# Per-token factors of an attention output: from widened transposes on TensorE to rows that go through DRAM

## The chip, the cores and the metric

The kernel runs on one core of a Trainium2 chip. The metric is the device time of one execution, in microseconds (us); the kernel before takes 1531.06 us in the median of three runs (1530.86 to 1531.6). TensorE is called PE here, VectorE DVE, ScalarE ACT, GpSimd POOL and SyncE SP, as in the profile. SP, ACT and POOL also issue DMAs, each in the order of its own queue.

## What is computed

Two layers of an encoder over 512 tokens with 1024 channels, in float32. Cut to what the change touches:

```python
proj = einsum('bsd,de->bse', x, w_in)                 # q, k, v of both mixers and two gates
oa, _ = banded_attention(qa, ka, va, 128, a_sink)     # mixer A: 8 heads, o / denom per token and head
ya = einsum('bse,ed->bsd', oa, w_branch_a)
for g, (window, dil) in enumerate(B_GROUPS):          # mixer B: 3 groups of 4 heads
    o, lse = dilated_attention(qb[g], kb[g], vb[g], window, dil)
wts = softmax(stack(lses), axis=0)                    # one factor per token, head and group
ob = einsum('gbsh,gbshd->bshd', wts, stack(outs))
yb = einsum('bse,ed->bsd', ob, w_branch_b)
h = einsum('bsd,de->bse', ga * ya + gb * yb, w_out)
x = layer_norm(alpha * x + h)
mlp = square(relu(x @ w_up)) @ w_down
x = layer_norm(alpha * x + mlp + sigmoid(x @ w_ple_gate + b) * (p[i] @ w_ple))
```

The change concerns the division by `denom` and the weights `wts`: a head's output `o` is kept with its 64 channels on the partitions and the 512 tokens along the row, so a factor per token has to be multiplied along the row, the same in 64 partitions.

## The kernel before

Weights come as 512 KB tiles `wst` through the SP queue into three buffers (L252), and are split into a high and a low part (`whi`, `wlo`; L236, or L240 with a POOL DMA that adds into `wlo`). Three matmuls per weight block (`mm3`, L287) make a float32 product out of the parts.

In `attention_block` (L358) PE's order is written by a planner: the loop at L854 runs small generators, each of which yields a condition on a forecast time `fc.t` and then emits the next step of a unit. Units of mixer A (`unit_a`, four per layer, two heads each) and of mixer B (`unit_b`, two spans `sp` times three groups `g`) emit scores (`sa`, `sb`), transposed probabilities (`pta`, `ptb`), and weighted values (`oa`, `ob`). Between them `filler` emits the projections (`ps_('qb', …)` and the like) and, at the end of the block, `ya`. `LEAVE` (L42) is a table by unit and step: a step listed there is put off by so many forecast microseconds after it could run. Only PE's order is fixed so; the other engines are put in order by the scheduler of the framework, which places each instruction where its own reckoning has the operands ready. Every engine and every queue then runs its list in order: what stands behind a waiting instruction waits too.

The scores of a step lie in two banks of tag `s`; DVE adds the mask into `pa` and takes the maximum (L466), which frees the bank; ACT takes the exponential (L462). Transposed probabilities go through two banks of tag `pt`, and are split by ACT and DVE. `o` is one bank, freed by `join` (L485: an ACT copy and a DVE addition).

The factors: `widened` (L493) copies a 128x8 tile of factors (tokens on the partitions) to 128x512 on ACT, 64 times each; `token_scaled` (L498) transposes its four 128x128 blocks into a `pt` bank (`rs`, L501) and DVE multiplies `f` by it (L502). A unit of mixer A does this once at its end, and `mix_b` (L704), once per span, three times, after the transposes `ex` and `ey` that bring the maxima and sums of the dilated groups into the order of the tokens. Then ACT and DVE split the result into `oah`/`oal` or `obh`/`obl`, which `ya` and `yb` read.

The embedding half `embedding(l, 0)` (L1096) for the second layer is made at the end of the first (L1358 to L1363) and kept in SBUF in the pool `p1` through the second layer's attention, until `embed` reads it. `kept` are DRAM tiles where the residual `y` waits meanwhile.

## Time and profile before

| | |
|---|---|
| profiled execution | 1530.95 us, of it 1529.2 us from the first to the last instruction |
| TensorE clock granted | 0.996 of full speed in the mean |
| attention of the first layer | about 38 to 305 us, of the second about 800 to 1068 us |
| end of the first layer, start of the second | about 750 to 790 us |
| DMA | 190.52 MB in the span, mean 125 GB/s |

Times inside the execution are microseconds from the first instruction. A matmul's duration reaches past the start of the next one, since matmuls are pipelined; what it costs PE is read from one start to the next.

### The profile page before, as it was taken

To read this page: it belongs to the slowest core of one execution; us is meant where nothing else is said; L and a number is where in the kernel's file an instruction comes from. 1 tells how busy PE (TensorE), PEld (TensorE's weight loads), DVE (VectorE), ACT (ScalarE), POOL (GpSimd) and SP (SyncE) were. 2 spreads that over 40 slices of the span, in tenths; PEclk is the share of its full clock that TensorE was granted. 3 is DMA by queue.
4 is the path that set the end of the run, shared out by engine and by line. 5 is a ranking of instruction groups with operands and counts; after the bars stand their busy time and mean duration, and the time that the engine had idled before them with its cause. 6 is when DMAs were issued, how large, how long until landed. Compare 5 with 4: busy or idle time off the path is not lost.

```text
span 1529.2 us, 19607 instructions
## 1 busy us (share of the span) xinstructions
PE 1506.9 (99%) x7374; PEld 1249.8 (82%) x7374; DVE 1030.7 (67%) x1761; ACT 768.2 (50%) x1254; POOL 250.9 (16%) x221
## 2 busy tenths in 40 slices
PE   9999999999999999999999999999999999999996
PEld 7888888888888888888888888888888888888885
DVE  5865564458568777686868655544585876767868
ACT  5887674344344443444558776643442444444342
POOL 1221220110011120202022112211100201111022
PEclk9999999999999999999999999999999999999998
DMA  7644655345612414151455456565455233231403
GB/s 243 144 109 117 147 138 191 99 138 152 206 56 86 135 53 155 42 159 62 105 169 138 113 123 150 126 188 156 150 151 181 69 110 111 85 123 56 150 0 97
DMA packets 54592, 190.52 MB, mean 125 GB/s; under 512 B 6625, under 2 KB 7009, under 8 KB 54497
## 3 DMA queue, kind: packets, MB, share of 16 engines
q1 hardware_dynamic: 43200, 151.74, 29.8%
q0 software_dynamic: 10576, 37.23, 13.0%
q8 instruction: 58, 0.95, 0.2%
q10 hardware_dynamic: 720, 0.30, 0.1%
q14 instruction: 38, 0.30, 0.1%
HBM read 155.16 MB, written 4.19 MB: 104 GB/s over the span
## 4 chain that ended last, share of the span: by engine, by line
PE 87%; DVE 6%; ACT 2%; DMA 2%; issue 2%; POOL 0%; SPq 0%; POOLq 0%; ACTq 0%; DVEq 0%
PE dn L1065 17%; PE ps_up L291 8%; PE ps_up L289 8%; PE ps_up L290 8%; PE wo L297 2%; PE pg L297 2%; PE pg L295 2%; PE pg L296 2%; PE wo L296 2%; PE wo L295 2%; PE pta L451 1%; PE sb L473 1%; PE sa L478 1%; PE ya L289 1%; PE ya L291 1%
## 5 line engine op out<-in xcount | busy, mean ns | idle before, releaser
L237 ACT CAST whi<-wst 128x1024 fp32r<-128x1024 f32 (+2 forms) x120 | 121.1, 1010 | 261.6 <-PE ps_up L290 115.4
L238 DVE TENSOR_TENSOR wlo<-wst,whi 128x1024 fp32r<-128x1024 f32 (+2 forms) x120 | 146.1, 1222 | 142.3 <-ACT whi L237 131.9
L289 PE MATMUL ps_up<-xhi,whi 128*128 128x512 f32 x512 | 199.2, 389 | 0.0
L290 PE MATMUL ps_up<-xlo,whi 128*128 128x512 f32 x512 | 199.2, 389 | 0.0
L291 PE MATMUL ps_up<-xhi,wlo 128*128 128x512 f32 x512 | 199.2, 389 | 0.0
L1038 POOL TENSOR_TENSOR hr<-r 128x512 f32<-128x512 f32 x64 | 102.2, 1597 | 550.2 <-ACT r L1030 529.7
L290 PEld LDWEIGHTS ps_up<-xlo,whi 128*128 128x128 f32 x512 | 96.1, 188 | 20.0
L291 PEld LDWEIGHTS ps_up<-xhi,wlo 128*128 128x128 f32 x512 | 96.1, 188 | 19.9
L289 PEld LDWEIGHTS ps_up<-xhi,whi 128*128 128x128 f32 x512 | 96.1, 188 | 19.9
L237 ACT CAST whi<-raw 128x1024 fp32r<-128x1024 f32 x56 | 58.0, 1052 | 97.0 <-PE ps_up L290 64.1
L237 ACT CAST dhi<-raw 128x1024 fp32r<-128x1024 f32 x56 | 58.7, 1052 | 82.2 <-PE dn L1065 59.5
L1084 DVE TENSOR_TENSOR y<-y,dn 128x512 f32<-128x512 f32 x96 | 65.2, 682 | 38.5 <-PE dn L1065 38.5
L244 POOL DMA_DIRECT2D wlo<-wst x54 | 47.8, 885 | 253.6 <-ACT wlo L243 150.9
L1018 DVE TENSOR_TENSOR raw<-raw,raw 128x1024 f32<-128x1024 f32 x64 | 86.4, 1350 | 0.2
L238 DVE TENSOR_TENSOR wlo<-raw,whi 128x1024 fp32r<-128x1024 f32 x56 | 68.2, 1220 | 14.1 <-ACT whi L237 14.1
L238 DVE TENSOR_TENSOR dlo<-raw,dhi 128x1024 fp32r<-128x1024 f32 x56 | 69.2, 1239 | 5.4 <-ACT dhi L237 5.4
L242 ACT CAST whi<-wst 128x1024 fp32r<-128x1024 f32 x54 | 56.5, 1046 | 30.3 <-PE ps_start L290 6.9
L243 ACT ACTIVATE wlo<-whi 128x1024 fp32r<-128x1024 f32 x54 | 57.3, 1061 | 0.8
L1065 PE MATMUL dn<-whi,smh 128*128 128x512 f32 x128 | 50.2, 394 | 0.7 <-DVE y L1084 0.7
L1065 PE MATMUL dn<-wlo,smh 128*128 128x512 f32 x128 | 50.5, 395 | 0.1
L1065 PE MATMUL dn<-whi,sml 128*128 128x512 f32 x128 | 49.9, 390 | 0.0
L1065 PE MATMUL dn<-dhi,smh 128*128 128x512 f32 x128 | 49.9, 390 | 0.0
(860 smaller groups left out, 4049.2 us busy)
## 6 DMA issues: line engine op xcount, KB each, us to landing
wst<-wst SPq DMA_DIRECT2D x187, 512.0 KB, 3.5
raw<-wst SPq DMA_DIRECT2D x64, 512.0 KB, 4.3
wlo<-wst POOLq DMA_DIRECT2D x54, 512.0 KB, 4.6
y<-rows POOLq DMA_DIRECT2D x14, 512.0 KB, 7.7
row<-rows SPq DMA_DIRECT2D x7, 512.0 KB, 8.4
wst<-wst SPq DMA_DIRECT2D x9, 256.0 KB, 2.7
xs<-xT SPq DMA_DIRECT2D x8, 256.0 KB, 6.2
y<-xN SPq DMA_DIRECT2D x4, 512.0 KB, 6.6
```

Source lines behind the costliest of these rows:

```text
L237: nc.scalar.copy(hi, src)
L238: nc.vector.tensor_tensor(lo, src, hi.bitcast(F32), ALU.subtract)
L289: nc.tensor.matmul(ps, w[0][:, s], x[0], start=start, stop=False, skip_group_check=part)
L290: nc.tensor.matmul(ps, w[0][:, s], x[1], start=False, stop=False, skip_group_check=part)
L291: nc.tensor.matmul(ps, w[1][:, s], x[0], start=False, stop=stop, skip_group_check=part)
L295: nc.tensor.matmul(ps, x[0], w[0][:, c], start=start, stop=False)
L296: nc.tensor.matmul(ps, x[0], w[1][:, c], start=False, stop=False)
L297: nc.tensor.matmul(ps, x[1], w[0][:, c], start=False, stop=stop)
L1018: nc.vector.tensor_tensor(to, to, other, ALU.add)
L1038: nc.gpsimd.tensor_tensor(h.rearrange("p s t -> p (s t)"), r, r, ALU.mult)
L1065: nc.tensor.matmul(ps[s], a[:, k, tok], w[b][:, cols], start=first and not (k or m), stop=k == 3 and m == 2, skip_group_check=True)
L1084: return nc.vector.tensor_tensor(to, to, ps, ALU.subtract if n in (2, 4, 5) else ALU.add)
```

## The change

For each unit of mixer A, and for each span of mixer B, one transpose turns the factors themselves (128x8, or 128x24 for three groups) into rows (`in_rows`). ACT copies the rows to SBUF and issues a DMA that writes them to a DRAM tile `line`. SP then reads a row of `line` back into 64 partitions, twice for a tile `R` of 128x512 (`in_columns`). The multiplication is taken out of the unit and put into a generator of its own on the list `side`, which waits until the forecast has passed `LATENCY` = 7 (`scaled_a`, `mixed_b`). `f` gets two buffers and `R` three; `ya` waits until all four `oa` are scaled. `LEAVE` has other entries.

The embedding half for the second layer is written to DRAM after it is made, and read back in `np1` in the second layer; no pool holds it through the attention.

```diff
+LATENCY = 7
 LEAVE = {
-    ("a", 0, 1): 0.6, ("a", 0, 14): 0.6, ("a", 1, 4): 0.3, ("a", 1, 16): 4.5, ("a", 2, 18): 1.0,
...
+    ("a", 0, 1): 2.2, ("a", 0, 11): 2.2, ("a", 0, 14): 1.5, ("a", 0, 16): 1.5, ("a", 1, 4): 1.0,
...
-            def widened(c, name, after):
-                wide = av.tile([P, 4, 2, 64], F32, tag="wide", name="wide" + name, bufs=1)
-                nc.scalar.copy(wide, c.rearrange("p r (j u) -> p j r u", u=1).to_broadcast([P, 4, 2, 64]))
-                return wide, fc.on("act", 0.52, after) + HOP
-
-            def token_scaled(f, wide, name, after):
-                R = bank("pt", "rs" + name)
-                for j in range(4):
-                    nc.tensor.transpose(R[:, j * P:(j + 1) * P], wide[:, j].rearrange("p r d -> p (r d)"), ident)
+            def in_rows(c, n, name, after):
+
+                tp = bank("pt", "rt" + name)
+                nc.tensor.transpose(tp[:n, :P], c, ident)
+                r = av.tile([24, P], F32, tag="rt", name="rt" + name, bufs=1)
+                nc.scalar.copy(r[:n], tp[:n, :P])
+                t = fc.on("act", 0.3, fc.pe(0.11) + HOP) + HOP
+                fc.take("pt", t)
+                line = dp.tile([24, P], F32, tag="line", name="line" + name, bufs=2)
+                nc.scalar.dma_start(line[:n], r[:n])
+                return line, max(t, after) + LATENCY
+
+            def in_columns(line, name):
+                R = av.tile([P, S], F32, tag="wide", name="R" + name, bufs=3)
+                for r in range(2):
+                    nc.sync.dma_start(R[r * 64:r * 64 + 64, :],
+                                      line[r * 4:r * 4 + 4].rearrange("j p -> (j p)").partition_broadcast(64))
+                return R
+
+            def scaled_a(i, f, R, t):
+                yield lambda: fc.t >= t
                 nc.vector.tensor_tensor(f, f, R, ALU.mult)
-                t = fc.on("dve", 0.6, max(fc.pe(0.43) + HOP, after)) + HOP
-                fc.take("pt", t)
-                return t
+                split(OA[i][0], OA[i][1], f)
+                forecast_split(S, fc.on("dve", 0.7, fc.t))
+                del held["oa", i]
+
+            def mixed_b(sp, fs, Rs, t):
+                yield lambda: fc.t >= t
+                for (f, _, _), R in zip(fs, Rs):
+                    nc.vector.tensor_tensor(f, f, R, ALU.mult)
+                f = fs[0][0]
+                nc.gpsimd.tensor_tensor(f, f, fs[1][0], ALU.add)
+                nc.vector.tensor_tensor(f, f, fs[2][0], ALU.add)
+                split(OB[sp][0], OB[sp][1], f)
...
-                yield lambda: fc.open("pt") and fc.t >= t_wide
-                t_f = token_scaled(f, wide, nm_, t_f)
-                split(OA[i][0], OA[i][1], f)
-                forecast_split(S, t_f)
+                yield lambda: fc.open("pt") and fc.t >= t_den
+                line, t = in_rows(den.rearrange("p r j -> p (r j)"), 8, nm_, t_f)
+                side.append([scaled_a(i, f, in_columns(line, nm_), t), None, ("oa", i), 0])
...
+                yield lambda: fc.t >= t and fc.open("pt")
+                line, t = in_rows(e.rearrange("p g b -> p (g b)"), 24, nm_, t)
+                Rs = [in_columns(line[8 * g:8 * g + 8], f"{nm_}_{g}") for g in range(3)]
+                side.append([mixed_b(sp, fs, Rs, t), None, ("ob", sp), 0])
...
-                        yield lambda: not any(k[0] == "a" for k in (*waiting, *live))
+                        yield lambda: not any(k[0] in ("a", "oa") for k in (*waiting, *live, *held))
...
+        kept_ple = [dp.tile([P, S], F32, tag=f"keptple{a}", name=f"keptple{a}", bufs=1) for a in range(4)]
...
+            for a in range(4 if l else 0):
+                ple[0, a] = np1.tile([P, S], F32, tag="ple0", name=f"ple{l}_0_{a}", bufs=4)
+                nc.sync.dma_start(ple[0, a], kept_ple[a])
...
+                    for a in range(4):
+                        nc.sync.dma_start(kept_ple[a], ple[0, a])
```

What this makes of the engines' lists is shown at three places, first before, then after the change.

The first place is PE's list where the first span's weights of mixer B are turned (first layer, second span under way). `rs_0_0` are the widened transposes, `rt_0` is the one transpose of the changed kernel; `ps_('vb', 1, 1)` and `ps_('qb', 1, 2)` are projections of the filler. Before:

```order
L483 MATMUL ob_1_0_0_2137<-ptlb_1_0_1_2068,vvvb_1_0_1927 64x2x128
L501 MATMUL rs_0_0_2166<-ident,wide_0_0_2102 128x128 x4
L289 MATMUL ps_('vb', 1, 1)_2124<-xhi,whi_1896 128x512
L290 MATMUL ps_('vb', 1, 1)_2124<-xlo,whi_1896 128x512
L291 MATMUL ps_('vb', 1, 1)_2124<-xhi,wlo_1897 128x512
L451 MATMUL ptb_1_0_3_2177<-ident,pb_1_0_1_1954 128x128 x4
```

After:

```order
L293 MATMUL ps_('vb', 1, 1)_2113<-xhi,wlo_1906 128x512
L498 MATMUL rt_0_2156<-ident,e_0_2045 24x128
L291 MATMUL ps_('qb', 1, 2)_2180<-xhi,whi_1997 128x512
L292 MATMUL ps_('qb', 1, 2)_2180<-xlo,whi_1997 128x512
L293 MATMUL ps_('qb', 1, 2)_2180<-xhi,wlo_1998 128x512
```

Before, three groups of four transposes stand within 23 rows of the list, the first of them shown; now one row stands there, between products of the filler.

The second place is DVE's list around the multiplication of mixer A's unit 1 (first layer). `pa_3_…<-sa_3_…` are the masks of unit 3's scores, `ptla_2_…` the low halves of unit 2's probabilities. Before:

```order
L466 ISA pa_3_1_994,mxa_3_995<-sa_3_0_1_1000,ct_157 128x256
L466 ISA mxa_3_995 128x1
L502 TENSOR_TENSOR fa_1_716<-fa_1_716,rsa_1_985 128x512
L532 SCALAR_TENSOR_TENSOR nma_3_996<-mxa_3_995,nsk_160 128x2
L238 TENSOR_TENSOR ptla_2_0_1019<-pta_2_0_1013,ptha_2_0_1018 128x512
L466 ISA pa_3_0_993,mxa_3_995<-sa_3_1_0_1049,ct_157 128x384
```

After:

```order
L240 TENSOR_TENSOR ptla_2_1_1043<-pta_2_1_1038,ptha_2_1_1042 128x384
L468 ISA pa_3_0_996,mxa_3_998<-sa_3_1_0_1052,ct_158 128x384
L468 ISA mxa_3_998 128x1
L516 TENSOR_TENSOR fa_1_713<-fa_1_713,Ra_1_993 128x512
L468 ISA pa_3_1_997,mxa_3_998<-sa_3_1_1_1053,ct_158 128x384
L468 ISA mxa_3_998 128x1
L555 SCALAR_TENSOR_TENSOR nma_3_999<-mxa_3_998,nsk_161 128x2
L240 TENSOR_TENSOR oal_152<-fa_1_713,oah_151 128x512
L240 TENSOR_TENSOR ptla_2_2_1079<-pta_2_2_1074,ptha_2_2_1078 128x384
```

The multiplication now reads `Ra_1`, which two DMAs bring, and stands between the masks of the two banks of `sa_3_1`; before, it read the bank that PE had just written.

The third place is SP's queue between the layers, with the writes of `y` and of the embedding half and the load of the constants `ct` for the second layer's attention. Before:

```order
L1355 DMA kept_136<-y_0_2869 128x1024
L366 DMA ct_6775<-cst 128x1920
L1355 DMA kept_137<-y_1_2870 128x1024
L258 DMA wst_6704<-wst 128x1024
L258 DMA wst_6839<-wst 128x1024
```

After:

```order
L1374 DMA kept_136<-y_0_2866 128x1024
L1374 DMA kept_137<-y_1_2867 128x1024
L1384 DMA keptple_140<-ple_0_0_6468 128x512
L260 DMA wst_6704<-wst 128x1024
L1384 DMA keptple_141<-ple_0_1_6477 128x512
L260 DMA wst_6840<-wst 128x1024
L1384 DMA keptple_142<-ple_0_2_6518 128x512
L1384 DMA keptple_143<-ple_0_3_6527 128x512
L368 DMA ct_6776<-cst 128x1920
```

`ct` has moved behind the four writes of the embedding half and two loads of weights.

## The prediction

> **What bounds the kernel now.** The page's busy times come first.

> ```profile
> PE 1506.9 (99%) x7374; PEld 1249.8 (82%) x7374; DVE 1030.7 (67%) x1761; ACT 768.2 (50%) x1254; POOL 250.9 (16%) x221
> ```

> Then the shares of the chain that ended last, by engine:

> ```profile
> PE 87%; DVE 6%; ACT 2%; DMA 2%; issue 2%; POOL 0%; SPq 0%; POOLq 0%; ACTq 0%; DVEq 0%
> ```

> PE is busy for 1506.9 of 1529.2 us, so the time falls only by work taken off PE or by its waits. The view of who waited for whom, for PE alone, gives the waits:

> ```profile
> PE ps_start L291 <- DMA wlo<-wst: 1.5, 1, 1.5
> ...
> PE sa L478 <- DVE mxa L466: 0.9, 2, 0.5
> ...
> PE rs L501 <- ACT wide L495: 0.8, 2, 0.4
> PE ptb L451 <- ACT pb L462: 0.4, 2, 0.2
> ```

> None is above 1.5 us. A late result costs more than the idle time shown, since the pipeline runs dry too; so I read costs from one start to the next, in PE's timeline; first around the first group of widened transposes:

> ```profile
> 71.94 0.34 PE L483 MATMUL oa<-ptla,vvva 128*64 128x384 f32 x1
> 72.12 0.60 PE L501 MATMUL rsa<-ident,widea 128*128 128x128 f32 x4
> 72.47 0.36 PE L478 MATMUL sa<-qh0ka,qh_qa 128*128 128x256 f32 x1
> ```

> Then around the first group of mixer B:

> ```profile
> 196.87 0.28 PE L482 MATMUL ob<-pthb,vvvb 128*128 128x256 f32 x1
> 196.98 0.28 PE L483 MATMUL ob<-ptlb,vvvb 128*64 128x256 f32 x1
> 197.68 0.65 PE L501 MATMUL rs<-ident,wide 128*128 128x128 f32 x4 [0.42 <-ACT wide L495]
> 198.09 0.48 PE L289 MATMUL ps_('vb', 1, 1)_2124<-xhi,whi 128*128 128x512 f32 x1
> ```

> And the last group:

> ```profile
> 1014.39 0.60 PE L501 MATMUL rs<-ident,wide 128*128 128x128 f32 x4
> 1014.74 0.48 PE L289 MATMUL ps_('g', 0, 6)_9225<-xhi,whi 128*128 128x512 f32 x1
> ```

> **What leaves PE.** Twenty groups of four widened transposes go: ten per layer, the first at 72.12, the last at 1014.39. Each steps 0.35 us (72.12 to 72.47), two 0.41: 7.1 us. With them goes the wait for `wide`: 196.98 to 197.68 is 0.70 where such a product takes 0.11, so 0.6, in both layers: 1.2 us.

> **What comes.** Twelve transposes of 128x8 or 128x24. The nearest rows are in two tile views: `rs`,

> ```profile
> L501 PE MATMUL rs<-ident,wide x48: 270/272/328, 197.7 to 1014.7; 128*128 128x128 f32 x48
> ```

> and `ex`, which turns 128x8 already:

> ```profile
> L713 PE MATMUL ex<-ident,cs x16: 272/273/276, 179.1 to 1002.5; 128*8 128x128 f32 x16
> ```

> The durations are equal, so I give the small one the step of the wide, 0.35/4 = 0.09: 1.1 us. If PE paid the 272 ns of the rows for each, 68 transposes fewer would save 18.5 us in place of 6.0; but four pass in 0.35 us, and I go by the steps. [...]

> **What moves with the table.** PE's timeline at two waits of the first layer, at the first scores of unit 0:

> ```profile
> 38.66 0.39 PE L291 MATMUL ps_('g', 0, 0)_403<-xhi,wlo 128*128 128x512 f32 x1
> 38.89 0.28 PE L478 MATMUL sa<-qh0ka,qhqa 128*128 128x256 f32 x1
> 39.39 0.39 PE L478 MATMUL sa<-ql0ka,qhqa 128*128 128x256 f32 x1 [0.23 <-DMA ql0ka<-ql0ka]
> 39.61 0.28 PE L478 MATMUL sa<-qh1ka,qlqa 128*128 128x256 f32 x1
> 39.94 0.39 PE L478 MATMUL sa<-ql1ka,qlqa 128*128 128x256 f32 x1
> ```

> and at the last of unit 1:

> ```profile
> 65.61 0.28 PE L478 MATMUL sa<-ql0ka,qhqa 128*128 128x256 f32 x1
> 66.37 0.38 PE L478 MATMUL sa<-qh1ka,qlqa 128*128 128x256 f32 x1 [0.47 <-DVE mxa L466]
> ```

> The first scores of unit 0 wait for DMAs that fill `ql0ka` and `ql1ka`: 0.50 and 0.33 in place of 0.11, 0.6 us. The new order puts nine more projection products ahead of them, 9 x 0.23 = 2.1 us (38.66 to 38.89 is one): the wait goes, 1.2 us in two layers. At 65.61 unit 1's last scores wait 0.65 for DVE's mask of the scores before; those move ahead of four transposes, so 0.35 of it goes, 0.7 in two layers. Against that, in unit (0, 2) of mixer B the transposes stand only 4.2 us of PE work behind the scores instead of 7.6. The two waits `ptb <- pb` stand where that distance is 3.5 and 3.8; I charge 0.4 per layer, +0.8 (between 0 and the 0.7 that `sa` loses at 65.61, per layer).

> **Between the layers.** SP's timeline has the load of the constants:

> ```profile
> 757.08 0.38 SPq L366 DMA_DIRECT2D ct<-cst  x1
> ```

> PE's timeline has the first products of the second layer, and the view of tile `wlo` the landing times of its additions:

> ```profile
> 765.79 0.28 PE L290 MATMUL ps_start<-xlo,whi 128*128 128x256 f32 x1
> 767.57 0.39 PE L291 MATMUL ps_start<-xhi,wlo 128*128 128x256 f32 x1 [1.50 <-DMA wlo<-wst]
> DMA to landing us min/median/max: 4.5/4.6/10.6
> ```

> PE waits 1.5 us for the DMA that adds into `wlo`. It normally lands in 4.6 us, here in 10.6: the load of `ct` starts within the same microsecond and shares the DMA engines. In the new order `ct` stands behind the writes of the embedding half, which exist only after PE's products up to 765.7. So the addition should land some 4 us sooner, and 1.5 us go. What is late next is the second half of `y`, which PE turns 6 us further on; it bounds nothing there now. `ct` is read only when the whole `start` projection ends, about 22 us later (96 products of 0.23).

> The read-back of the embedding half (four DMAs, 1 MB) stands in SP's queue after the `y` loads of the second layer; weights issued behind it have five tiles' work of PE, over 25 us, in hand. Cost 0; if the cover failed, one weight tile would come late by the 1 MB's share of the queue, some 4 us.

> **The way through DRAM.** This is the unknown. PE waits for `R` nowhere itself: `ya` and `yb` come tens of microseconds later. But DVE runs in order, and the multiplication waits at its place in DVE's list. The place that counts is the one shown for unit 1: behind the multiplication stands the mask of the second bank of `sa_3_1`, which the next scores need. The rows for each leg: the landing lines of the tile views of `sk` (4 KB from DRAM, on ACT's queue), `ql0ka` and `qh0ka` (128 KB), in this order;

> ```profile
> DMA to landing us min/median/max: 1.5/2.7/3.9
> DMA to landing us min/median/max: 2.4/2.5/2.7
> DMA to landing us min/median/max: 5.1/5.3/5.5
> ```

> then, from the views of `gate` and `rsa`, the page's groups and DVE's timeline, ACT's gate, DVE's multiplication, ACT's cast of weights and DVE's mask:

> ```profile
> L894 ACT ACTIVATE gate<-ps_('g', 0, 2)_934,vhalf x1: 687/687/687, 94.8 to 94.8; 128x512 f32<-128x512 f32 x1
> L502 DVE TENSOR_TENSOR fa<-fa,rsa x8: 677/680/685, 74.3 to 901.0; 128x512 f32<-128x512 f32 x8
> L242 ACT CAST whi<-wst 128x1024 fp32r<-128x1024 f32 x54 | 56.5, 1046 | 30.3 <-PE ps_start L290 6.9
> 97.19 0.55 DVE L466 CUSTOM_DVE_ANT_0 pa<-sa,ct 128x384 f32<-128x384 f32 x1
> ```

> Count from PE's small transpose. ACT copies the row, but in its list a cast of weights (1.05 us, free to start when PE leaves a gate projection at +0.8) and that gate's activation (0.69) stand ahead of the DMA: it is issued at about +2.8. The write takes 2.7, SP's two issues 0.4 till the second starts, the read 2.5: `R` is there at +8.4. By the order of the changed kernel PE comes to the second bank of the next scores after 21 products of 0.23, 14 transposes of 0.09, 8 products of 0.11 and 8 of 0.18 (71.94 to 72.12): +8.4. Ahead of that DVE must multiply (0.68) and mask (0.55), so `R` was due at +7.1: 1.3 us late, and 0.6 more for the low halves queued behind. In unit 0 the join of `oa_1_0` stands behind the multiplication, with a split between: `R` at about +8.2 makes it some 0.8 late. Units 2 and 3 and both spans of mixer B have 3 us or more of PE work in hand behind the multiplication: 0. So 2.7 a layer, **+5.4**. The ends: with a write of 1.5 and a read of 2.4 `R` comes at +7.1 and costs nothing; with 3.9 and 5.3 at +12.4, 4.0 more than I take, which unit 0, unit 1 and the first span pay each, 2 x (2.7 + 3 x 4.0) = 29.

> [...]

> ACT loses twenty copies and gains twelve small ones, DVE's count is the same; neither ends a wait by that. Twelve lines put 40 more issues on SP (eight units of two, four spans of six), each under 0.5 us; where one waits for its `line`, the weights queued behind wait too, again with over 25 us in hand: 0.

> **The sum.** -7.1 - 1.2 + 1.1 - 1.2 - 0.7 + 0.8 - 1.5 + 5.4 = -4.4. The profiled execution took 1530.95 us (1529.2 of span and 1.75 around it), 0.1 under the median of the runs: **1526.6 us**.

> **Rivals.**
> - *The rows come in time.* `R` at +7.1 or before: the sum without 5.4, 1521.2, and about 1519 if the new table spares the charge of 0.8 and the `ptb` waits too. For it: the quick legs in the rows. Against: DMA is never long idle in the attention. 17%.
> - *Slower: DVE waits for the read-back.* If the read is as slow as `qh0ka` (5.3), `R` is at +11.2; each of three places per layer pays 2.8 more, 16.8 in all: 1543. It decides at about +9.1, where 4.4 are eaten up. For it: weight loads use the same queue, and the engines share them. Against: the reads are issued where the weights before them have mostly landed. 10%.
> - *Nothing gained.* `R` at +9.1, or other waits of the new order as large as those removed (3.1): 1530 to 1534. 13%.
> - *Transposes cost their full duration.* 18.5 us leave with them in place of 6.0: 1514. Against: the steps of 0.35. 2%.

> **How the numbers follow.** The forecast, 1522.5 to 1530, has 58%. The range of 1519 to 1533 holds it, most of the first rival and most of the third. A measurement tells 0.2% from no change, 3.1 us. Faster by more (under 1528.0): the first and fourth rival and 0.41 of the forecast, 0.60. Within: 0.17 + 0.13 = 0.30. Slower: 0.10.

> **What would show it.** PE's busy time lower by about 6 us; no wait of PE for `wide`, `ql0ka` or, after the layers' border, `wlo`; DVE idle before the multiplication of units 0 and 1 with the DMA named as its releaser, and a wait of `sa` for DVE after it. Wrong would be: PE waits at `ya`, `yb` or for weights, or DVE idle for the read-back in mixer B.

## The result, and the profile after

| | us |
|---|---|
| kernel after, median of 5 runs | 1537.77 (1536.53 to 1538.79) |
| kernel before, median of 5 runs beside it | 1530.86 (1529.04 to 1531.6) |
| ratio, with its 95% interval | 1.0048 (1.0037 to 1.006) |
| profiled execution after | 1538.79, of it 1537.0 from the first to the last instruction |

The change makes the kernel 0.5% slower, about 7 us; 1526.6 was predicted. The page of the kernel after, busy times first, then the chain that ended last by engine:

```profile
PE 1504.0 (98%) x7306; PEld 1243.8 (81%) x7306; DVE 1027.3 (67%) x1761; ACT 759.2 (49%) x1246; POOL 252.3 (16%) x221
...
PE 82%; DVE 6%; DMA 6%; ACT 3%; issue 1%; SPq 1%; POOL 0%; DVEq 0%; POOLq 0%; ACTq 0%
```

PE has less to do (1506.9 before), and DMA, 2% of the chain before, is 6% of it now. The view of who waited for whom says where, first for PE, then for DVE (engine, tile and line that waited, what it waited for; us in total, times, longest):

```profile
PE sa L480 <- DVE mxa L468: 5.5, 2, 2.8
PE ob L484 <- DVE ogb L490: 2.6, 1, 2.6
PE ptb L453 <- ACT pb L464: 2.1, 2, 1.0
...
PE ob L485 <- DVE ptlb L240: 1.5, 1, 1.5
PE ob L714 <- DVE ogb L490: 1.3, 2, 0.7
...
PE ps_('g', 1, 3)_9517 L293 <- DVE wlo L240: 0.5, 1, 0.5
PE ps_('g', 1, 3)_9517 L291 <- ACT whi L239: 0.4, 1, 0.4
```

```profile
DVE fa L516 <- DMA Ra<-linea: 29.7, 8, 5.2
...
DVE ogb L524 <- DMA R<-line: 22.1, 7, 6.9
```

The waits for `wide`, `ql0ka` and `wlo` at the border are gone, as forecast. In their place PE waits for DVE: for masks (`mxa`), for joins (`ogb` L490), for splits (`ptlb`). And DVE idles 52 us for `R`, in all eight units and all four spans. One of these chains, unit 1 of the first layer, in the timelines of PE, ACT, SP and DVE (start, duration, engine and line, operation; in brackets the idle time ahead and its releaser):

```profile
90.69 0.27 PE L498 MATMUL rta<-ident,dena 128*8 128x128 f32 x1
...
99.36 0.34 PE L480 MATMUL sa<-ql0ka,qh_qa 128*128 128x384 f32 x1
102.45 0.44 PE L480 MATMUL sa<-qh1ka,ql_qa 128*128 128x384 f32 x1 [2.76 <-DVE mxa L468]
```

```profile
91.83 0.26 ACT L500 COPY rta<-rta 8x128 f32<-8x128 f32 x1
91.99 1.04 ACT L244 CAST whi<-wst 128x1024 fp32r<-128x1024 f32 x1
92.11 0.28 ACTq L504 DMA_DIRECT2D linea<-rta  x1
```

```profile
91.22 0.33 SPq L260 DMA_DIRECT2D wst<-wst  x1
94.97 1.09 SPq L510 DMA_DIRECT2D Ra<-linea  x2
```

```profile
96.13 0.55 DVE L468 CUSTOM_DVE_ANT_0 pa<-sa,ct 128x384 f32<-128x384 f32 x1
...
101.23 0.69 DVE L516 TENSOR_TENSOR fa<-fa,Ra 128x512 f32<-128x512 f32 x1 [4.54 <-DMA Ra<-linea]
101.84 0.55 DVE L468 CUSTOM_DVE_ANT_0 pa<-sa,ct 128x384 f32<-128x384 f32 x1
```

PE's transpose starts at 90.69, ACT issues the line's DMA 1.42 later, SP starts to issue the reads at +4.3, and DVE multiplies at +10.5. The mask of the second bank stands behind, and PE, ready for the next scores at 99.7, gets on at 102.45.

PE then goes on slowly. The windows of that stretch (busy us of PE, PEld, DVE, ACT and POOL, then the clock granted to PE, the DMA share and GB/s):

```profile
98.00:100.00 2.00, 1.70 (x11) 1.20 (x9) 0.00 (x0) 0.00 (x0) 0.14 (x2) 1.00 0.92 200
100.00:102.00 2.00, 0.00 (x0) 0.00 (x0) 0.77 (x2) 0.04 (x1) 0.00 (x0) 1.00 0.14 24
102.00:104.00 2.00, 1.55 (x7) 1.21 (x8) 1.95 (x6) 2.00 (x6) 0.00 (x0) 0.91 0.71 250
104.00:106.00 2.00, 2.00 (x8) 1.73 (x7) 2.00 (x7) 1.95 (x6) 0.00 (x0) 0.50 0.01 4
106.00:108.00 2.00, 2.00 (x11) 1.76 (x11) 1.65 (x5) 1.97 (x6) 0.75 (x1) 0.74 0.00 0
```

Behind the wait PE's clock is halved for 3.4 us. This comes three times, each 3.4 us long: here, at 216 behind the wait of 2.60 for the join, at 868 behind the other wait for `mxa` (2.73). Windows of 1 us, added up from 10 to 1517 us as (1 - clock), give 5.1 us lost, and 0.0 in the kernel before.

### The profile page after: what moved, and what is told of

It reads as the page before. It is cut to its first block, busy times and chain, and to the rows that moved or that the text cites. A ratio compares the mean times of both kernels' runs of the same rounds, so it can differ in the third digit from the quotient of the medians.

```text
span 1537.0 us, 19552 instructions
## 1 busy us (share of the span) xinstructions
PE 1504.0 (98%) x7306; PEld 1243.8 (81%) x7306; DVE 1027.3 (67%) x1761; ACT 759.2 (49%) x1246; POOL 252.3 (16%) x221
## 4 chain that ended last, share of the span: by engine, by line
PE 82%; DVE 6%; DMA 6%; ACT 3%; issue 1%; SPq 1%; POOL 0%; DVEq 0%; POOLq 0%; ACTq 0%
PE dn L1082 17%; PE ps_up L291 8%; PE ps_up L293 8%; PE ps_up L292 8%; PE pg L299 2%; DMA wst<-wst 2%; PE wo L299 2%; PE wo L297 2%; PE wo L298 2%; PE pg L297 2%; PE pg L298 2%; DMA Ra<-linea 1%; DMA R<-line 1%; PE sb L475 1%; PE ps_start L292 1%
## 5 line engine op out<-in xcount | busy, mean ns | idle before, releaser
L291 PE MATMUL ps_up<-xhi,whi 128*128 128x512 f32 x512 | 199.2, 389 | 0.0
L291 PEld LDWEIGHTS ps_up<-xhi,whi 128*128 128x128 f32 x512 | 96.1, 188 | 19.9
L299 PE MATMUL pg<-bhi,xlo 128*128 128x512 f32 x128 | 49.9, 390 | 0.3 <-DVE xlo L979 0.3
```

Of the source, the lines that this page charges most:

```text
L291: nc.tensor.matmul(ps, w[0][:, s], x[0], start=start, stop=False, skip_group_check=part)
L299: nc.tensor.matmul(ps, x[1], w[0][:, c], start=False, stop=stop)
```

## The experiments

The theory, T: the loss is DVE's wait for the read-back at the multiplications' places in its list, what PE then waits for, and the halved clock. The rivals: U, the new table's order, or the extra DMAs as such; V, the way through DRAM costs wherever the multiplication stands; W, a multiplication put off further holds up something else. Each run was timed beside the kernel before on the same chip; its medians there were 1530.25 (first four), 1530.43 (e5 to e8) and 1530.81 (e9 to e12).

**Is it the wait for the line?** e1_constant_rows:

```diff
-                                      line[r * 4:r * 4 + 4].rearrange("j p -> (j p)").partition_broadcast(64))
+                                      rows[l, 0][0:512].partition_broadcast(64))
```

> The read into R takes a row of the input that lies in DRAM from the start, in place of the line just written; so the factors applied are others, and the output is not the reference's. The line is still written, the number and size of the DMAs and PE's order are those of the changed kernel; only what R waits for is gone. Theory T (the loss is DVE's wait in order for the read-back, with what PE then waits for and the low clock behind the long waits): PE's waits for masks, joins and splits after the multiplications go (2.92 + 2.77 + 2.90 + 1.61 + 0.91 + 0.74 = 11.9 us between starts), and with them three stretches of about 4 us at half the clock, some 2 us each lost in the two longest, 4 to 5 in all: 1521 us, between 1518 and 1524, and no PE wait above 1.6 us outside the start. Rival U (the new table's order, or the extra DMA load on queues and engines, is to blame): the waits stay and the time is 1533 to 1538.

Measured: 1520.74 us (1519.75 to 1522.0), ratio 0.9935 (0.9923 to 0.9948). PE's longest waits now:

```profile
PE ptb L453 <- ACT pb L464: 2.0, 2, 1.0
PE dn L1082 <- DVE y L1101: 1.3, 4, 0.4
```

As T said: every wait behind a multiplication is gone and DVE waits for `R` nowhere. The same number of DMAs of the same size, in the same PE order, leaves no wait of this kind; the dependence on the line costs 17 us (1.0048 - 0.9935 of 1530). U falls. DVE's list differs too: with early data the multiplications stand a few places sooner in it, so this run alone does not part the late data from the place; the next one moves the place alone.

**Can the multiplication just stand later?** e2_later_in_list (`last_on_dve` finds the last DVE instruction traced; `mixed_b` has the same, with its three multiplications):

```diff
             yield lambda: fc.t >= t
-            nc.vector.tensor_tensor(f, f, R, ALU.mult)
-            split(OA[i][0], OA[i][1], f)
             forecast_split(S, fc.on("dve", 0.7, fc.t))
             del held["oa", i]
+            yield lambda: fc.t >= t + 4
+            with tc.issue_after(last_on_dve()):
+                nc.vector.tensor_tensor(f, f, R, ALU.mult)
+            split(OA[i][0], OA[i][1], f)
...
```

> The computation is the reference's. The twelve places of multiplications are put off in DVE's own list: each is traced when the planner's clock stands 4 us further on, and must be issued behind the last DVE instruction traced until then. PE's order is unchanged row by row, the way through DRAM too. Theory T: DVE idles for R under 1 us at each place in place of 2.0 to 6.9, PE's waits behind it go, and the clock holds: 1522 us, between 1519 and 1526, faster than both kernels. Rival V (the way through DRAM as such, its receipts and queue slots, costs the time): 1533 to 1538, waits only move. Rival W (the multiplications, later, now hold up something else: the buffers f and ogb, or ACT's casts, which run in order): a new PE wait for ACT or DVE of 2 us or more, 1526 to 1533.

Measured: 1526.22 us (1525.31 to 1528.3), ratio 0.9973 (0.9962 to 0.9983): faster than both kernels, 0.2 us above the range that T gave. DVE never waits for `R`. V falls, and W holds in part, by these new waits of PE:

```profile
PE ps_('g', 1, 4)_9582 L291 <- ACT gate L921: 1.8, 1, 1.8
PE ob L723 <- DVE ogb L490: 1.8, 2, 0.9
```

The first span's three multiplications stand ahead of the second span's first join; and at the end of layer 1, a gate comes late.

**The embedding half alone.** e3_embedding_only is the kernel before with the change's lines on `kept_ple`, `ple` and `p1` and nothing else of it.

> The kernel before with the embedding half through DRAM alone; factors and table as before. My step for the layers' border: PE's wait for the addition into wlo (1.5 us) goes, since the constants' load stands behind the writes; 1529.4 us against 1530.9. Rival X (the read-back of 1 MB delays the weights of the projections that follow, as the changed kernel's late weights of gate (1,3), 0.58 + 0.69 us, suggest): the border gains 1.5 to 1.8 and the weights lose 1.3, 1530 to 1531; if the late weights are larger here, slower than before.

Measured: 1530.52 us (1528.98 to 1531.05), ratio 0.9999 (0.999 to 1.0008). In its profile, of the fastest of its eleven runs, PE does not wait for `wlo` at the border nor for late weights, and the span is 1527.2 us against 1529.2 before. The medians don't show that gain: the interval reaches from 1.5 us faster to 1.2 slower. So the wait goes, but whether 1.5 us are gained stays open.

**The table alone.** e4_old_table is the kernel after with the table `LEAVE` of before.

> The changed kernel with the table of put-off steps of the kernel before. Theory T: the multiplications stand where DVE's list puts them whatever the table, DVE waits 2 to 6 us for R at most of them, PE waits behind: 1533 to 1543, and PE's waits that the new table removed (the low halves of ka at the first scores, 0.6 a layer) are back. Rival U (the new table is to blame): 1526 or less.

Measured: 1549.78 us (1548.31 to 1552.6), ratio 1.0127 (1.0113 to 1.0141). PE's waits, then DVE's timeline where the first of them arises:

```profile
PE ptb L452 <- ACT pb L463: 11.8, 2, 6.3
PE yb L290 <- ACT gate L910: 4.8, 1, 4.8
```

```profile
141.31 0.08 DVE L467 DVE_READ_ACCUMULATOR2_ANT mxb<- 128x1 f32 x1
146.78 0.69 DVE L515 TENSOR_TENSOR fa<-fa,Ra 128x512 f32<-128x512 f32 x1 [5.39 <-DMA Ra<-linea]
...
148.32 0.16 DVE L664 TENSOR_SCALAR cs<-mxb 128x4 f32<-128x4 f32 x1
```

Here a multiplication stands between the last masks of a unit and the small step (L664) that its exponentials need, and PE waits for those. U falls once more: the new table is worth 12 us to the changed kernel, since it decides what stands behind the reader of `R`. T had the sign, and its range ended 7 us too low.

**A shorter end of the attention.** e5_end_not_put_off has e2's edit with these times for `mixed_b`:

```diff
-                yield lambda: fc.t >= t + 4
-                with tc.issue_after(last_on_dve()):
+                yield lambda: fc.t >= t + (0 if sp else 8)
+                with ExitStack() if sp else tc.issue_after(last_on_dve()):
```

> As the run with the multiplications later in DVE's list (1526.2 us), but the last span's multiplications of each layer stand as in the changed kernel, and the first span's 8 us later in place of 4, so that the join of the next span's first group goes ahead of them. PE's order is the same. Theory T: the two waits for that join (1.05 and 1.07 us between starts) go; and since the attention's buffers come free earlier at a layer's end, the loads that reuse them, with the weights queued behind them, come earlier: the wait of 1.98 us at gate (1,4) of layer 1 falls to 1.3 or below. 1522 to 1524 us. Rival W (a multiplication put off always holds up something of like size): 1525 to 1528.

Measured: 1524.96 us (1523.33 to 1525.07), ratio 0.9955 (0.9942 to 0.9967), 1 us above T's range and at the lower edge of W's. The join is on time and the wait at gate (1,4) is gone, but of the buffers `og`, four in number, the second span's group 1 needs one that the first span still reads:

```profile
PE ob L723 <- ACT ogb L725: 2.0, 2, 1.0
```

**Is the embedding's read-back what makes weights late there?** e6_read_back_late moves its four DMAs behind `projected(a, 0, pss[a])`, held behind the SP instructions traced until then.

> As e5_end_not_put_off, and the read-back of the embedding half (four DMAs, 1 MB) stands in SP's queue behind the weights of the output projection's second half, where it is still ahead of its first reader. Theory Q (weights are late at the end of layer 1's attention since 1 MB more stands ahead of them in the queue): no PE wait at the gates (1,3) and (1,4), up to 1.5 us less than e5, 1520.5 to 1523. Rival (the loads of y and the rows, which were there before, are what the weights wait for): the same as e5 within 0.5 us.

Measured: 1529.58 us (1525.15 to 1532.52, 12 runs), ratio 0.9987 (0.9977 to 0.9996), slower than e5; the profile is of the fastest run. Both expectations fall. PE still waits, 3.2 us at gate (1,2), where ACT, in order, waits 6.23 for a weight tile; y, `pf` and the rows were issued just ahead of it. Why most runs are slower than the profiled one was not looked into.

**Is SP's queue to blame for the late `R`?** e7_reads_on_gpsimd puts `nc.gpsimd.dma_start` in the place of `nc.sync.dma_start` in `in_columns`.

> The changed kernel with the reads into R issued by GpSimd in place of SP; DVE's and PE's order are the list's of the changed kernel or close to it. If SP's queue (issues of 0.45 to 0.91 us, one behind the other, and behind a weight load) makes R late: R comes 0.5 to 1 us sooner, each wait behind it shrinks by as much, 1531 to 1535. If it is the write and the read themselves: 1536 to 1539. If the wait for the line holds up the additions into weights that GpSimd issues: PE waits for wlo, above 1540.

Measured: 1544.47 us (1540.37 to 1547.66), ratio 1.0084 (1.0069 to 1.0099). DVE's waits for `R` don't shrink in sum (53.4 us in place of 51.8):

```profile
DVE fa L516 <- DMA Ra<-linea: 32.2, 8, 7.4
DVE ogb L524 <- DMA R<-line: 21.2, 5, 7.1
```

So taking the reads off SP's queue brings `R` no sooner. How much SP's own slots cost stays open, since the reads that GpSimd issues took longer themselves: they landed after 4.9 and 5.3 us in the median (4.4 and 4.8 on SP). PE's waits changed as well. In the profiled run, the slowest of the six, those for `mxa` are gone, those for joins come to 5.3 us in place of 3.9, one of 9.15 us stands at gate (1,2) of layer 1, where ACT waits 11.85 us for weights, and the clock loses 10.2 us in place of 5.1. The wait for `wlo` that I had named does not appear. What makes those weights so late was not tried.

**What does an idle of PE do to its clock?** e8_idle_lengths, in the kernel before:

```diff
                             mm3(ps, w, k, x, k == 0, k == KT - 1)
+                            if i == 3 and k == 3:
+                                for n in ((6, 10, 14, 18), (22, 26, 34, 42))[l][q], 0:
+                                    nc.tensor.matmul(warm2[:88, :32], rgap, wgap, start=True, stop=True)
+                                    for _ in range(n):
+                                        nc.gpsimd.memset(wgap, 0.0)
```

> The kernel before with eight planted waits of PE in the up projections, four in each layer: a product that waits for a chain of memsets on GpSimd (6, 10, 14, 18, 22, 26, 34 and 42 of them, estimated at 0.12 us each from the memset of 128x32 in the profile, so 0.7 to 5 us). Theory C (an idle of 2.6 us or more drops the granted clock to a half for about 4 us, one of 1.5 us or less does not): the clock stays 1.00 behind the first two and falls to 0.5 behind the waits above 2.6 us, each of which then costs some 2 us beyond its idle time. Rival (the low clock in the attention had another cause): 1.00 behind all.

Measured: 1592.62 us, a single run. A memset and its turn took longer than I had estimated, so the waits are 1.23, 3.09, 3.82, 4.55, 4.15, 6.01, 7.47 and 8.94 us. PE's timeline behind the second, then the windows (columns as above):

```profile
535.50 0.34 PE L1255 MATMUL warm<-wgap,rgap 128*88 128x32 f32 x2 [3.09 <-POOL wgap L1257]
...
537.45 0.63 PE L289 MATMUL ps_up<-xhi,whi 128*128 128x512 f32 x1
537.88 0.63 PE L290 MATMUL ps_up<-xlo,whi 128*128 128x512 f32 x1
```

```profile
535.00:537.00 2.00, 1.50 (x7) 1.27 (x8) 0.00 (x0) 0.00 (x0) 0.33 (x3) 0.94 0.00 0
537.00:539.00 2.00, 2.00 (x6) 1.58 (x5) 0.00 (x0) 0.00 (x0) 0.00 (x0) 0.50 0.00 0
```

Products of 128x512 step 0.43 in place of 0.23. Theory C holds here: no loss behind 1.23 us, and behind each of the other seven waits the steps beyond 0.23 add up to some 1.6 to 2.9 us. The low clock is the idle's doing, not the attention's; what its length alone does not settle stands in the last section.

**Taking the buffers away from e5.** e9_more_buffers:

```diff
-                f = av.tile([P, S], F32, tag="og", name="og" + nm_, bufs=4)
+                f = av.tile([P, S], F32, tag="og", name="og" + nm_, bufs=6)
```

> As e5_end_not_put_off (1525.0 us), with six buffers for the outputs of mixer B's groups in place of four, so that no group of the second span waits for the first span's multiplications to give a buffer back. Theory W of before, now as the mechanism (in e5 ACT's copy of the second span's group 1 waits for the buffer that GpSimd's sum of the first span still reads, and PE waits 1.18 and 1.17 us between starts for that copy): both waits go, 1522.6 us, between 1521 and 1524. If another wait takes their place: 1525.

Measured: 1521.56 us (1519.53 to 1525.81), ratio 0.9941 (0.9929 to 0.9952). Both waits go, so the buffers were what held PE up there (W). In the time, the two intervals overlap.

**Whose share is it?** In e10_units_constant the row of the input is read where the tile's name begins with `a`, in e11_last_span_only in the first spans too; else the line.

> The changed kernel, with the factors of mixer A's units read from a row of the input that lies in DRAM from the start; mixer B's come from the written line. The output is not the reference's. What goes is the units' share: their two waits (2.92 and 2.90 us between starts) and the two stretches of half clock behind them, some 2 us each by the planted waits (1.6 to 2.8 lost behind each wait above 3 us): 1528 us, between 1525.5 and 1530. If the units' waits are harmless and mixer B's carry the loss: above 1533.

Measured: 1529.52 us (1528.76 to 1531.05), ratio 0.9993 (0.9984 to 1.0002).

> As e10_units_constant, and the first span's factors come from the input too; only the last span of each layer waits for its line. Against e10 the first span's share goes (2.77 + 1.61 + 0.91 + 0.74 us between starts and one stretch of half clock, some 2): 1521 to 1523. What remains above 1520.7, the time with all factors from the input, is the last span's share: the loads that reuse the attention's buffers wait for its multiplications, and the weights of gate (1,3) behind them come 1.3 us late: 1522. If my step of no cost for the last span was right: 1520.7 within 0.5.

Measured: 1521.41 us (1520.52 to 1521.92), ratio 0.9936 (0.9924 to 0.9948). By ratios of 1530: the units of mixer A cost 8.4 us (1.0048 - 0.9993), the first spans 8.7 (0.9993 - 0.9936), the last spans 0.2 (0.9936 - 0.9935), each with about 2 us of uncertainty. Both times lie within what was expected. The 1.3 us expected for the last spans are in e11's trace as waits at gate (1,3), but not to be told apart in the time.

**Moving what crowds the layer's end.** e12_y_later is e9 with the loads of y, and the additions into it, behind the second of the four steps of the loop over `bb`.

> As e9_more_buffers, and in both layers the loads of y (2 MB, with 2 MB of additions into it in the second) are issued behind the weights of the second quarter of mixer B's gates, in place of at the end of the attention. Theory: the bunch of loads at the layer's end makes weights late there, so the waits at gate (1,3) (0.64 + 0.69 us between starts in e5) go: 1.3 us less than e9, 1521 us. If y comes late in their place, PE waits at the output projection or later: as e9 or slower.

Measured: 1520.41 us (1519.48 to 1521.49), ratio 0.993 (0.9918 to 0.9942). No gate waits any more; against e9 the time is 1.1 us less, with intervals that overlap. This is the best version, 0.7% faster than the kernel before and 1.2% faster than the change as it was made.

## Why the prediction was wrong

**What leaves PE, the small transposes, the table's moves, the border** (in sum -9.8) came out right together: they give 1530.95 - 9.8 = 1521.2, and with the read-back's wait out of the way e1 took 1520.7. That is luck in part, since singly they are off. PE's busy time fell by 9.7 in e1 (1506.9 to 1497.2), where I had said 6; the rest of PE's span, its waits, fell by 1.5 (22.3 to 20.8), where I had said 3.8. The waits for `wide` and for the low halves of `ka` are gone, and unit 1's last scores wait no more at all. In unit (0, 2) of mixer B nothing new shows; `ptb` waits in the second span, 1.0 in place of 0.2. For the border see e3. The rival in which a transpose costs its full duration is out: 1514 was not reached in e1.

**The way through DRAM** (+5.4) is the step that failed; the runs make it 17 us. From start to start, both layers together, unit 1 pays 5.8 us (I had 3.8), unit 0 nothing (I had 1.6), the first span 6.0 (I had nothing), and the clock 5.1 (I had no term).

- *"`R` is there at +8.4"*: it was +10.5 in unit 1. The line's DMA went out at +1.4, not +2.8: it was issued at 92.11, while the cast ahead of it in ACT's list ran until 93.0 and the gate had not begun (92.94). SP issued the two reads at +4.3 and +4.8; by my count it would have been +5.5 and +5.9. But the slower of the two took 5.7 us, where I had put 2.5. The landing lines of `Ra` in this unit (94 to 102 us), then of all tiles `Ra` and `R`:

```profile
DMA to landing us min/median/max: 3.8/4.7/5.7
DMA to landing us min/median/max: 3.3/4.4/5.7
DMA to landing us min/median/max: 3.1/4.8/7.3
```

 The range of my bounds, 2.4 to 5.3, held the medians, and I took its lower end, from `ql0ka`'s row: a copy within SBUF that GpSimd issues, not a read of DRAM on SP's queue. The DMA engines are 92% busy from 98 to 100 us, while this read is under way; that the load makes it slow no run shows.

- *"In unit 0 the join of `oa_1_0` stands behind the multiplication"*: DVE idles 2.06 there, and PE waits for nothing, in either layer. Unit 1 is as I described it, with 2.92 and 2.90 us from start to start in place of 1.9.

- *"Units 2 and 3 and both spans of mixer B have 3 us or more of PE work in hand"*: so the units, but not the first span. Six reads and three multiplications in a row hold up the second span's first join until 214.63 (the last of the three multiplications took 1.69 us in place of 0.69; why was not looked into). PE waits 2.60 in layer 0, and for a split and joins in layer 1. That share, 8.7 us by e10 and e11 with its stretch of low clock, I had at nothing. DVE idle for the read-back in mixer B, which I had named as a sign of being wrong, came: 22.1 us.

- *The halved clock*, 5.1 us, is in no term: I priced a wait at its length.

The slower rival had this mechanism with a 10% chance: at +11.2 each of three places per layer pays 2.8 more, 1543. Put at +10.5 (2.1 more), its own working gives 1521.2 + 5.4 + 6 x 2.1 = 1539.2; 1537.8 was measured. It was right that the read is slow and that PE pays behind it. That its time is so near is luck: of its three places a layer unit 0 pays nothing, where its working has 5.8 us for the two layers, and the clock's 5.1, which it has in no term, takes their place.

**Weights "with over 25 us in hand"** was wrong too, if small. SP's timeline at the end of layer 1's attention, before and after, then DVE's after:

```profile
1016.78 3.79 SPq L1128 DMA_DIRECT2D y<-kept  x4
```

```profile
1023.18 3.64 SPq L510 DMA_DIRECT2D R<-line  x6
1030.86 0.33 SPq L260 DMA_DIRECT2D wst<-wst  x1
1031.31 1.78 SPq L1145 DMA_DIRECT2D y<-kept  x4
```

```profile
1029.00 0.69 DVE L524 TENSOR_TENSOR ogb<-ogb,R 128x512 f32<-128x512 f32 x1 [6.89 <-DMA R<-line]
1029.61 1.22 DVE L240 TENSOR_TENSOR wlo<-wst,whi 128x1024 fp32r<-128x1024 f32 x1
```

The loads of y stand in SP's queue behind the six reads of `R` and a load of weights. That load waits 4.0 us for DVE's split of an earlier weight tile (1029.61), which frees its buffer; and the split stands behind a multiplication that waits 6.89 us for `R`. The loads of y start 14.5 us later than before, while PE is 5.8 us behind there (its last `ya` starts at 1041.5 in place of 1035.7); the weights behind them are late by 0.58 and 0.69 from start to start at gate (1,3). e12 takes the crowd away, and these waits go.

## What to carry to other kernels

A round trip through DRAM was cheap here while nothing needed its end (e9, with the trip, took 1521.56 us; e1, where nothing waits for the line, 1520.74): so look at what stands behind its reader in that engine's list, and put the reader past the trip's slow end, with buffers enough that nobody waits for it in turn. Price it by the slowest nearby landing, not by the quickest. And look at what a wait of PE costs beside its length: those of 2.60, 2.73 and 2.76 us after the change cost 1.7 us each in clock (5.1 in all).

## What the hardware showed beside it

In these runs the length of an idle alone doesn't say whether the clock falls. Waits of 1.23 us (e8) and 1.50 (the kernel before, at 767) left it at 1.00, and every planted wait from 3.09 to 8.94 halved it; of the waits that were not planted, 1.82 us did so in e2 (clock 0.50 from 1056 to 1058), as did 2.60, 2.73 and 2.76 after the change, and 3.22 in e6 did not (1.00 throughout).

When the clock changed can be worked out from the traces. The starts and the ends of the three stretches after the change follow from the windows in which they lie (columns as above):

```profile
103.00:104.00 1.00, 1.00 (x6) 0.66 (x5) 1.00 (x3) 1.00 (x4) 0.00 (x0) 0.82 0.67 262
107.00:108.00 1.00, 1.00 (x7) 0.86 (x7) 1.00 (x3) 0.97 (x2) 0.75 (x1) 0.98 0.00 0
216.00:217.00 1.00, 1.00 (x5) 0.76 (x5) 1.00 (x3) 1.00 (x2) 0.00 (x0) 0.64 0.00 0
219.00:220.00 1.00, 1.00 (x4) 0.81 (x3) 0.49 (x1) 0.00 (x0) 1.00 (x2) 0.66 0.00 0
868.00:869.00 1.00, 0.68 (x2) 0.68 (x3) 0.96 (x4) 1.00 (x3) 0.00 (x0) 0.61 0.83 287
871.00:872.00 1.00, 1.00 (x6) 0.91 (x5) 0.39 (x3) 0.67 (x2) 0.00 (x0) 0.68 0.00 0
```

A mean of 0.82 means 0.36 us at half, so the first start is 103.64; the others are 216.28 and 868.22. The ends are 107.04, 219.68 and 871.64, so the stretches are 3.40, 3.40 and 3.42 us long. The starts lie 112.64 and 651.94 us apart, 33 and 191 times 3.413. The fall behind the last product, at 1526.99, lies 658.77 behind the third start, 193 times 3.413:

```profile
1526.98:1527.00 0.02, 0.00 (x0) 0.00 (x0) 0.02 (x1) 0.02 (x1) 0.02 (x1) 0.78 1.30 205
```
